# A two-layer network in one kernel: the layer's output kept in SBUF over the layer change, operand sums on one engine, an output projection begun earlier

## The chip, the cores and the metric

The kernel runs on one core of a Trainium2 chip. The metric is the device time of one execution in microseconds (us). Lower is better. Before the change it is 2079.74 us, the median of three runs (2078.81 to 2080.0).

## The reference, cut to what matters

One sequence of 1024 tokens with 1024 features goes through two layers in float32. The first (even) layer mixes by pooling, retention and attention to a memory of 256 tokens; the second (odd) by block-sparse attention with 12 heads ("NSA") and again by attention to the memory.

```python
def even_layer(h, mem_n, g, w_in, pool_w, pool_scale, w_mem_kv, w_out):
    u = rmsnorm(h, g)
    za, rq, rk, rv, xq, gate = split_cols(u @ w_in, EVEN_SPLITS)
    ...
    y = jnp.concatenate([a, r, m], axis=-1) * jax.nn.silu(gate)
    return h + y @ w_out

def odd_layer(h, mem_n, g, w_in, cmp_pe, cmp_w1, cmp_b1, cmp_w2, w_mem_kv, w_out, rel_bias):
    u = rmsnorm(h, g)
    q, kc, vc, ks, vs, kw, vw, gl, xq, gate = split_cols(u @ w_in, ODD_SPLITS)
    c = nsa_attention(q, kc, vc, ks, vs, kw, vw, gl, cmp_pe, cmp_w1, cmp_b1, cmp_w2, rel_bias)
    m = mem_attention(xq, mem_n, w_mem_kv)
    y = jnp.concatenate([c, m], axis=-1) * jax.nn.silu(gate)
    return h + y @ w_out
```

The change touches three places: the end of the first layer (`h + y @ w_out`), the start of the second (`rmsnorm`, and the operands of `u @ w_in`), and the start of the second layer's attention.

## The kernel before, in words

Activations are kept transposed, features on the 128 partitions and tokens along the free dimension, in two halves of 512 tokens (`hf` 0 and 1); a tensor of 1024 features is 8 tiles of 128x512 per half. PE (TensorE) does every product of a weight and an activation as three matmuls of 512 columns (L77 to L79), because each operand is split into a high part, which ACT casts (L70), and a low part, the difference, which DVE (VectorE) or POOL (GpSimd) computes (L71). A weight is loaded raw as `wr`, split into `wh` and `wl`, and then used.

The order in which each engine takes its instructions is not written out by hand: the program is traced in the order of the code, a scheduler reorders it with a model of times, and each engine then runs its own list strictly in order. DMAs are nearly all issued from SP's list, in order as well. Where an instruction waits, everything behind it on its engine waits too.

**The layer change.** `out_proj` (from L538, loop over `ct`, 8 output tiles) computes the first layer's output: 24 matmuls per tile into `ps_mm`, plus the residual `xr` (loaded from `hp`), stored to DRAM as `hd`; squares are summed into `hacc` for the norm. While the second half's `out_proj(1)` runs on PE, the first half is loaded from `hd`, scaled in place by its norm (L764), split into the operands B11 and B21, and stored again, scaled, to `xd` (L757 to L768).

The odd layer's projections multiply both halves of the tokens and both halves of the features by a scheme of the Strassen kind, with 7 products in place of 8 (`strassen`, L225). Its activation operands are B11, B21 (of the first half alone), B22 (of the second half alone) and T1 to T4 (sums and differences of both). `u_half` (L174) scales a half by its norm and makes the operands that need that half alone; `u_sums` (L181) makes T1 to T4. Six column groups (kc, vc, q0, q2, q4, q6) are begun with B11 and B21 alone (`early`, L203), 12 products of 12 matmuls each. Their order: the six `early` groups; then `mem_kv` (L295), the second layer's keys and values of the memory, which depends on nothing in the stream; then `u_half` of the second half and `u_sums`. The second half is loaded back from `hd`, the first from `xd`, 16 loads. `strassen` then goes through kc, vc, q and the rest, with weight sums `ws` on POOL (L231 to L234).

**The start of attention.** After the last projection, `kv_prep(0)` brings the keys and values, then `scores` of unit 0 (a head of a half) are computed, then for every unit `values` beside the next unit's `scores`. `od_out` (L831) is a generator of output products y·w (12 matmuls per step, 8 per half for this group), whose first group of four heads comes from the memory attention (`ymr` loaded from `ymd`). `proj_step` (L1262) takes one of its steps; it is called from the loop over units, so first beside unit 0's values.

## Time and profile before

| | |
|---|---|
| time, median of 3 runs | 2079.74 us (2078.81 to 2080.0) |
| the profiled execution's own time | 2074.93 us |
| its span in the trace | 2073.1 us |
| PE busy | 1945.5 us, 94% of the span |
| DVE, ACT, POOL busy | 1281.2, 943.2, 614.2 us (62%, 45%, 30%) |
| mean granted PE clock | 0.967 of full speed |
| DMA | 273.36 MB, 132 GB/s over the span |

The rows further down have, for an instruction, its start in us, its duration, engine, line, operation and tiles (output<-inputs), and in brackets how long the engine stood idle before it and what released it. A granted clock of 0.50 means that PE ran at 1.2 GHz in place of 2.4 GHz. Line numbers are those of the kernel before.

### The profile page before, as it was taken

The numbers are of one execution on the slowest core, as the hardware profiler recorded it, in microseconds if no ns is written. First come the engines' busy times: TensorE is split into PE (matmuls) and PEld (weight loads), VectorE is DVE, ScalarE is ACT, GpSimd is POOL, SyncE is SP. The second block draws the span as 40 slices with busy tenths as digits, with TensorE's granted clock in tenths as the row PEclk, the third lists the DMA queues.
The fourth block names the chain that finished last, engine by engine and source line by source line (L and its number), as shares of the span: only waits on it lengthen the run. The fifth ranks groups of instructions, "written<-read, shape, count | busy, mean of one in ns | idle before, by whom it ended". The sixth has DMA issues, their size and how long they took to land.

```text
span 2073.1 us, 28764 instructions
## 1 busy us (share of the span) xinstructions
PE 1945.5 (94%) x9814; PEld 1618.8 (78%) x9814; DVE 1281.2 (62%) x2729; ACT 943.2 (45%) x1867; POOL 614.2 (30%) x627
## 2 busy tenths in 40 slices
PE   5799999979999999849999999998999999999997
PEld 4688888858888877728878788886788888878885
DVE  4666465555655563484536965676575677767675
ACT  4444332334432243331123344545575677756664
POOL 0121110010311002174436643342344443333422
PEclk9899999989999999959999999999999999999998
DMA  6423234442232438517645443335536442152312
GB/s 202 155 81 102 82 110 134 160 138 92 84 104 82 157 130 279 191 47 219 211 129 164 157 136 129 129 120 182 190 120 203 161 132 62 34 166 62 108 41 91
DMA packets 131702, 273.36 MB, mean 132 GB/s; under 512 B 15927, under 2 KB 33091, under 8 KB 131523
## 3 DMA queue, kind: packets, MB, share of 16 engines
q1 hardware_dynamic: 131556, 271.53, 40.7%
q8 instruction: 77, 1.26, 0.3%
q14 instruction: 69, 0.57, 0.1%
HBM read 211.16 MB, written 62.66 MB: 132 GB/s over the span
## 4 chain that ended last, share of the span: by engine, by line
PE 48%; DVE 4%; POOL 2%; DMA 2%; issue 1%; ACT 1%; SPq 0%; DVEq 0%; POOLq 0%; ACTq 0%
PE ps_t L120 5%; PE ps_a L77 3%; PE ps_a L78 3%; PE ps_a L79 3%; PE ps_s L77 3%; PE ps_s L79 3%; PE ps_s L78 3%; PE ps_mm L79 3%; PE ps_mm L77 3%; PE ps_mm L78 3%; PE ps_o L84 2%; PE ps_o L82 2%; PE ps_o L83 2%; PE ps_b L77 2%; PE ps_b L79 2%; PE ps_b L78 2%
## 5 line engine op out<-in xcount | busy, mean ns | idle before, releaser
L70 ACT CAST wh<-wr 128x512 fp32r<-128x512 f32 (+1 forms) x395 | 242.2, 618 | 474.5 <-PE ps_mm L78 304.4
L71 DVE TENSOR_TENSOR wl<-wr,wh 128x512 fp32r<-128x512 f32 (+1 forms) x281 | 208.1, 745 | 175.9 <-ACT wh L70 168.9
L77 PE MATMUL ps_mm<-uh,wh 128*128 128x512 f32 x640 | 253.2, 398 | 2.7 <-ACT uh L70 2.7
L79 PE MATMUL ps_mm<-uh,wl 128*128 128x512 f32 x640 | 252.9, 395 | 0.0
L78 PE MATMUL ps_mm<-ul,wh 128*128 128x512 f32 x640 | 252.6, 395 | 0.0
L71 POOL TENSOR_TENSOR wl<-wr,wh 128x512 fp32r<-128x512 f32 x114 | 150.0, 1318 | 325.7 <-ACT wh L70 270.4
L79 PE MATMUL ps_mm<-yh,wl 128*128 128x512 f32 x512 | 205.4, 402 | 2.2 <-DVE wl L71 1.3
L77 PE MATMUL ps_mm<-yh,wh 128*128 128x512 f32 x512 | 203.2, 403 | 4.0 <-ACT wh L70 2.1
L78 PE MATMUL ps_mm<-yl,wh 128*128 128x512 f32 x512 | 204.4, 400 | 0.2 <-DVE yl L71 0.2
L71 DVE TENSOR_TENSOR apl<-ps_t,aph 128x512 fp32r<-128x512 f32 x204 | 135.9, 671 | 44.0 <-ACT aph L70 38.6
L70 ACT CAST aph<-ps_t 128x512 fp32r<-128x512 f32 x204 | 114.5, 567 | 86.7 <-PE ps_o L83 44.5
L77 PEld LDWEIGHTS ps_mm<-uh,wh 128*128 128x128 f32 x640 | 121.1, 190 | 28.3 <-ACT uh L70 4.4
L78 PEld LDWEIGHTS ps_mm<-ul,wh 128*128 128x128 f32 x640 | 121.1, 189 | 24.6 <-DVE ul L71 0.5
L79 PEld LDWEIGHTS ps_mm<-uh,wl 128*128 128x128 f32 x640 | 120.9, 189 | 24.6
L1201 POOL TENSOR_TENSOR Pw<-Pw,arc 128x640 f32<-128x640 f32 (+2 forms) x96 | 97.7, 1018 | 141.1 <-DVE arc L1197 65.4
L70 ACT CAST wh<-ws 128x512 fp32r<-128x512 f32 x88 | 54.2, 619 | 136.0 <-PE ps_a L78 63.0
L77 PEld LDWEIGHTS ps_mm<-yh,wh 128*128 128x128 f32 x512 | 95.7, 188 | 25.3 <-ACT wh L70 4.5
L79 PEld LDWEIGHTS ps_mm<-yh,wl 128*128 128x128 f32 x512 | 96.3, 188 | 24.0 <-POOL wl L71 2.6
L78 PEld LDWEIGHTS ps_mm<-yl,wh 128*128 128x128 f32 x512 | 96.3, 188 | 20.3 <-DVE yl L71 0.8
L71 DVE TENSOR_TENSOR wl<-ws,wh 128x512 fp32r<-128x512 f32 x88 | 71.2, 811 | 40.8 <-ACT wh L70 37.6
L1193 ACT ACTIVATE Ps<-Ps,anm 128x512 f32<-128x512 f32 (+3 forms) x96 | 74.6, 777 | 27.0 <-DVE anm L1190 26.7
L1203 ACT ACTIVATE Ps<-Ps,arc 128x512 f32<-128x512 f32 (+3 forms) x96 | 74.4, 777 | 21.6 <-DVE arc L1197 20.0
(891 smaller groups left out, 4863.6 us busy)
## 6 DMA issues: line engine op xcount, KB each, us to landing
wr<-in_ev_gate SPq DMA_DIRECT2D x32, 512.0 KB, 3.5
wr<-in_ev_out SPq DMA_DIRECT2D x32, 512.0 KB, 3.6
wr<-in_od_out SPq DMA_DIRECT2D x64, 256.0 KB, 3.2
oa<-oho SPq DMA_DIRECT2D x52, 256.0 KB, 2.5
oxr<-oa SPq DMA_DIRECT2D x52, 256.0 KB, 2.8
x<-in_xT SPq DMA_DIRECT2D x32, 256.0 KB, 3.7
wr<-in_od_q SPq DMA_DIRECT2D x16, 512.0 KB, 3.9
w<-in_cmp_w SPq DMA_DIRECT2D x16, 512.0 KB, 4.8
```

The lines of the kernel that those rows point to most:

```text
L70: act.copy(hi, src)
L71: (eng or dve).tensor_tensor(lo, src, hi.bitcast(F32), OP.subtract)
L77: pe.matmul(o, wh, xh, start=start, stop=False, skip_group_check=skip)
L78: pe.matmul(o, wh, xl, start=False, stop=False, skip_group_check=skip)
L79: pe.matmul(o, wl, xh, start=False, stop=stop, skip_group_check=skip)
L82: pe.matmul(o, wh, xh, start=start, stop=False)
L83: pe.matmul(o, wl, xh, start=False, stop=False)
L84: pe.matmul(o, wh, xl, start=False, stop=stop)
L120: pe.transpose(o, x, ident[:k, :k])
L1193: act.activation(pt, pt, AF.Exp, bias=nm[:, bi:bi + 1], accum_out=su[:, bi:bi + 1])
L1201: pool.tensor_tensor(pt, pt, rc[:, bi:bi + 1].to_broadcast(list(pt.shape)), OP.mult)
L1203: act.activation(pt, pt, AF.Copy, scale=rc[:, bi:bi + 1])
```

## The change: what it does

1. **The halves stay in SBUF.** A pool `xp` with 16 tiles X[f][k] is opened ahead of `out_proj(1)`. The first half's X[0] is loaded from `hd` and scaled in place by `u_half`; nothing is stored to `xd`. For the second half, `out_proj` loads the residual into X[1][ct] and adds the product in place, so that the half is in SBUF when the norm is known. 24 DMAs of 256 KB are gone: 8 stores to `xd`, 8 loads from it, 8 loads from `hd`. The squares get a tile of their own, `hsq`.
2. **Order and engines of the operands.** `u_half` of the second half and `u_sums` stand behind the first two `early` groups, ahead of the other four and of `mem_kv`. In `u_sums` every subtraction and every split's low half is on DVE (before, POOL had 8 subtractions and 4 of the splits' low halves, with T4's splits on DVE). T4's splits come after `mem_kv` (`u_last`).
3. **Start of attention.** One `proj_step` stands ahead of `kv_prep(0)`, and one in each step of unit 0's `scores`.
4. Pools are opened earlier or on the other side, and the tile `th` of a gate comes from another pool with two buffers.

```diff
@@ out_proj @@
-                    xr = ep.tile([128, HT], F32, name="xr", tag="xr", bufs=2)
+                    last = hf == 1 and not first
+                    xr = X[1][ct] if last else ep.tile([128, HT], F32, name="xr", tag="xr", bufs=2)
                     sp.dma_start(xr, a["xT"][ct][:, hf * HT:(hf + 1) * HT] if first else hp_[ct][hf])
-                    t = ep.tile([128, HT], F32, name="ho", tag="ho", bufs=2)
+                    t = xr if last else ep.tile([128, HT], F32, name="ho", tag="ho", bufs=2)
                     dve.tensor_tensor(t, o, xr, OP.add)
@@ u_sums @@
             dve.tensor_tensor(b11, b12, b11, OP.subtract)
-            pool.tensor_tensor(b12, b22, b12, OP.subtract)
+            dve.tensor_tensor(b12, b22, b12, OP.subtract)
             dve.tensor_tensor(b22, b22, b11, OP.subtract)
             split(*U["T2"][k], b22)
-        for k in range(4):
-            split(*U["T3"][k], x[1][k], eng=(dve, pool)[k % 2])
-        for k in range(4):
-            split(*U["T1"][k], x[0][k], eng=(dve, pool)[k % 2])
+            dve.tensor_tensor(x[0][k + 4], x[0][k + 4], b22, OP.subtract)
+        for nm, f in (("T3", 1), ("T1", 0)):
+            for k in range(4):
+                split(*U[nm][k], x[f][k])
+
+    def u_last(U, uo, x):
         U["T4"] = u_late(uo)
         for k in range(4):
-            pool.tensor_tensor(x[0][k + 4], x[0][k + 4], x[1][k + 4], OP.subtract)
             split(*U["T4"][k], x[0][k + 4])
@@ layer change @@
     for k in range(8):
-        x = ep.tile([128, HT], F32, name="x0", tag="pa", bufs=3)
-        sp.dma_start(x, hd[k][0])
-        dve.scalar_tensor_tensor(x, x, gains[:, 1, k:k + 1], rb, OP.mult, OP.mult)
-        split(*U[("B11", "B21")[k // 4]][k % 4], x)
-        sp.dma_start(xd[k], x)
+        sp.dma_start(X[0][k], hd[k][0])
+    u_half(U, X, 1, 0, rh[0], tm2.tile([128, HT], F32, name="rb", tag="rb"))
     out_proj(1, EV_ORDER[1], False)
...
-        ahead = [("kc", 0), ("vc", 0), ("q", 0), ("q", 2), ("q", 4), ("q", 6)]
...
-            if n == 0:
-                for k in range(8):
-                    sp.dma_start(X[1][k], hd[k][1])
-                    sp.dma_start(X[0][k], xd[k])
-        drain(mem_kv("od", None, u_late(uo), wtile("mrb")[:, :NMEM]))
-        u_half(U, X, 1, 1, rh[1], wtile("rb"))
-        u_sums(U, uo, X)
+    ahead(("kc", 0), ("vc", 0))
+    u_half(U, X, 1, 1, rh[1], wtile("rb"))
+    u_sums(U, X)
+    ahead(("q", 0), ("q", 2), ("q", 4), ("q", 6))
+    drain(mem_kv("od", None, u_late(uo), wtile("mrb")[:, :NMEM]))
+    u_last(U, uo, X)
@@ attention @@
+        proj_step()
         kv_prep(0)
         res = []
         for _ in scores(*units[0], res):
-            pass
+            proj_step()
         kv_prep(1)
```

The scheduler moves more than the code does. Three places, in the rows of the engines' lists, each with its tiles' numbers and what it waits for:

DVE at the start of `out_proj(1)`, where the low halves of the weights of output tile 0 are done (`wl_6626` before, `wl_6630` now). Before:

```order
L71 TENSOR_TENSOR wl_6622<-wr_6619,wh_6621 128x512 [waits DMAHW6_49,Activation_49]
L71 TENSOR_TENSOR wl_6626<-wr_6619,wh_6625 128x512 [waits Activation_49]
L71 TENSOR_TENSOR B110l_6547<-x0_6571,B110h_6546 128x512 [waits Activation_49]
L71 TENSOR_TENSOR B111l_6549<-x0_6577,B111h_6548 128x512 [waits Activation_49]
L71 TENSOR_TENSOR wl_6664<-wr_6661,wh_6663 128x512 [waits DMAHW7_49,Activation_49]
L71 TENSOR_TENSOR wl_6668<-wr_6661,wh_6667 128x512 [waits Activation_49]
```

Now:

```order
L178 SCALAR_TENSOR_TENSOR x05_6571<-x05_6571,c_gains_66,rb_6590 128x512 [waits DMAHW7_49]
L71 TENSOR_TENSOR B112l_6552<-x02_6568,B112h_6551 128x512 [waits Activation_49]
L178 SCALAR_TENSOR_TENSOR x06_6572<-x06_6572,c_gains_66,rb_6590 128x512 [waits DMAHW0_49]
L178 SCALAR_TENSOR_TENSOR x07_6573<-x07_6573,c_gains_66,rb_6590 128x512 [waits DMAHW1_49]
L71 TENSOR_TENSOR B113l_6554<-x03_6569,B113h_6553 128x512 [waits Activation_49]
L71 TENSOR_TENSOR B210l_6556<-x04_6570,B210h_6555 128x512 [waits Activation_49]
L566 TENSOR_TENSOR x10_6574<-ps_mm_6633,x10_6574 128x512 [waits DMAHW2_49,PE_49]
L71 TENSOR_TENSOR B211l_6558<-x05_6571,B211h_6557 128x512 [waits Activation_49]
L71 TENSOR_TENSOR wl_6667<-wr_6664,wh_6666 128x512 [waits DMAHW3_49,Activation_49]
L71 TENSOR_TENSOR wl_6671<-wr_6664,wh_6670 128x512 [waits Activation_49]
```

Between the low halves of tile 0 and those of tile 1 (`wl_6664` before, `wl_6667` now) stood two splits; now there stand 14 instructions: 7 scalings, 6 splits and the sum of tile 0, which needs its 24 matmuls done. The last ten of the 16 rows are shown.

DVE ahead of `mem_kv`, whose first weights' low half is `wl_7399` before and `wl_7424` now (T40h to T43l at L306 and L308 are the memory's operand there, in T4's tiles). Before:

```order
L306 SCALAR_TENSOR_TENSOR T42h_7365<-wr_7380,c_gains_66,T42h_7365 128x256 [waits DMAHW7_49,Activation_49]
L306 SCALAR_TENSOR_TENSOR T42l_7366<-wr_7380,c_gains_66,T42l_7366 128x256 [waits Activation_49]
L306 SCALAR_TENSOR_TENSOR T43h_7367<-wr_7380,c_gains_66,T43h_7367 128x256 [waits Activation_49]
L306 SCALAR_TENSOR_TENSOR T43l_7368<-wr_7380,c_gains_66,T43l_7368 128x256 [waits Activation_49]
L71 TENSOR_TENSOR wl_7399<-wr_7396,wh_7398 128x512 [waits DMAHW0_49,PE_49,Activation_49]
```

Now:

```order
L189 TENSOR_TENSOR x05_6571<-x05_6571,x15_6579 128x512 [waits DVE_49]
L308 SCALAR_TENSOR_TENSOR T42h_7390<-wr_7405,c_gains_66,T42h_7390 128x256 [waits DMAHW7_49,Activation_49]
L308 SCALAR_TENSOR_TENSOR T42l_7391<-wr_7405,c_gains_66,T42l_7391 128x256 [waits Activation_49]
L308 SCALAR_TENSOR_TENSOR T43h_7392<-wr_7405,c_gains_66,T43h_7392 128x256 [waits Activation_49]
L71 TENSOR_TENSOR T21l_6991<-x15_6579,T21h_6990 128x512 [waits Activation_49]
L71 TENSOR_TENSOR T22l_6993<-x16_6580,T22h_6992 128x512 [waits Activation_49]
L189 TENSOR_TENSOR x06_6572<-x06_6572,x16_6580 128x512
L308 SCALAR_TENSOR_TENSOR T43l_7393<-wr_7405,c_gains_66,T43l_7393 128x256
L189 TENSOR_TENSOR x07_6573<-x07_6573,x17_6581 128x512 [waits DVE_49]
L71 TENSOR_TENSOR T23l_6995<-x17_6581,T23h_6994 128x512 [waits Activation_49]
L71 TENSOR_TENSOR wl_7424<-wr_7421,wh_7423 128x512 [waits DMAHW2_49,Activation_49,Pool_49]
```

All of `u_half` and `u_sums` now stands ahead of `mem_kv`'s first weights on DVE: from the first scaling of the second half to `T23l` 50 instructions, 8 scalings, 16 subtractions, 16 splits, 8 of the memory's operand and 2 sums of `early` groups. The T1 to T4 products need nothing further from DVE but T4's splits.

PE at the start of attention, behind the last projection's transposes of values. Before:

```order
L120 MATMUL ps_t_12545<-c_ident_72,vraw_12543 128x128 x3
L77 MATMUL ps_s_12606<-ks0h_12511,aqh_12594 128x512 [waits Activation_49]
L78 MATMUL ps_s_12606<-ks0l_12512,aqh_12594 128x512 [waits DVE_49]
L79 MATMUL ps_s_12606<-ks0h_12511,aql_12595 128x512 [waits Pool_49]
L77 MATMUL ps_s_12612<-kw0h_12515,aqh_12594 128x512 [waits Activation_49]
```

Now:

```order
L120 MATMUL ps_t_12547<-c_ident_72,vraw_12545 128x128 x3
L77 MATMUL ps_mm_12523<-yh_12501,wh_12519 128x512 [waits Activation_49]
L77 MATMUL ps_mm_12634<-yh_12501,wh_12630 128x512 [waits DVE_49]
L78 MATMUL ps_mm_12523<-yl_12502,wh_12519 128x512 [waits DVE_49]
L79 MATMUL ps_mm_12523<-yh_12501,wl_12520 128x512 [waits Pool_49]
L77 MATMUL ps_mm_12523<-yh_12505,wh_12519 128x512 [waits Activation_49]
```

Two output products, 24 matmuls, now stand ahead of unit 0's first score on PE. The matmuls ahead of unit 0's values are as many as before.

## Rows read from the trace of the kernel before

**Rows 1.** The page: the span, and the busy time, share and instructions of each engine.

```profile
span 2073.1 us, 28764 instructions
PE 1945.5 (94%) x9814; PEld 1618.8 (78%) x9814; DVE 1281.2 (62%) x2729; ACT 943.2 (45%) x1867; POOL 614.2 (30%) x627
```

**Rows 2.** Busy time by stage: the stretch, its length, then busy us (and count) of PE, PEld, DVE, ACT and POOL, the granted PE clock, the DMA engines' busy share, GB/s. The first stretch is the start of `out_proj(1)`, then come the `early` groups, `mem_kv`, the operands of the second half, the first Strassen groups, and the start of attention in two parts.

```profile
760.00:812.00 52.00, 46.99 (x200) 36.67 (x198) 32.83 (x50) 23.11 (x40) 6.21 (x5) 1.00 0.73 244
812.00:846.00 34.00, 30.49 (x130) 24.85 (x130) 7.41 (x15) 10.79 (x22) 10.22 (x9) 0.95 0.77 273
846.00:875.00 29.00, 28.43 (x168) 25.01 (x168) 14.06 (x24) 10.07 (x18) 0.24 (x1) 1.00 0.70 218
875.00:929.00 54.00, 19.72 (x39) 10.29 (x39) 44.86 (x50) 17.83 (x31) 40.47 (x21) 0.61 0.16 53
929.00:974.00 45.00, 45.00 (x192) 36.01 (x193) 17.71 (x28) 8.18 (x14) 17.27 (x13) 0.90 0.73 219
1425.00:1436.00 11.00, 5.86 (x17) 3.85 (x16) 6.00 (x12) 4.11 (x7) 2.55 (x2) 0.69 0.96 311
1436.00:1476.00 40.00, 34.07 (x165) 26.31 (x165) 25.04 (x66) 25.07 (x58) 21.56 (x24) 0.97 0.89 307
```

**Rows 3.** What PE waited for from 760 to 975 us: PE's tile and line, who released it, total us, times, the longest.

```profile
PE ps_b L77 <- ACT T10h L70: 8.4, 1, 8.4
PE ps_b L78 <- POOL T11l L71: 6.3, 1, 6.3
PE ps_b L78 <- DVE T10l L71: 5.2, 1, 5.2
PE ps_t L154 <- DVE dg L149: 4.4, 1, 4.4
PE ps_a L77 <- DVE u L242: 4.1, 1, 4.1
PE ps_a L78 <- DVE T20l L71: 2.9, 1, 2.9
PE ps_t L134 <- DVE hacc L128: 2.7, 1, 2.7
PE ps_s L77 <- ACT wh L70: 2.6, 1, 2.6
...
PE ps_a L79 <- DVE wl L71: 2.0, 1, 2.0
```

**Rows 4.** Short stretches, columns as in rows 2: one behind the wait at 813 us, one behind the wait at 846 us, three of the operands' stage.

```profile
816.00:818.00 2.00, 2.00 (x6) 1.51 (x6) 0.00 (x0) 0.00 (x0) 0.00 (x0) 0.50 1.00 368
844.00:848.00 4.00, 1.51 (x10) 1.30 (x11) 3.43 (x7) 2.73 (x6) 0.00 (x0) 1.00 0.41 110
880.00:900.00 20.00, 3.53 (x6) 1.13 (x4) 16.31 (x23) 8.69 (x15) 13.47 (x5) 0.50 0.16 53
900.00:920.00 20.00, 11.37 (x22) 5.90 (x22) 20.00 (x13) 6.51 (x11) 20.00 (x12) 0.59 0.00 0
920.00:940.00 20.00, 15.13 (x50) 11.14 (x51) 8.88 (x16) 2.94 (x5) 4.76 (x4) 0.67 0.36 113
```

**Rows 5.** DVE, in order of time: a step of the memory's operand, then scalings of the second half, subtractions, and a split of T2.

```profile
836.26 0.48 DVE L306 SCALAR_TENSOR_TENSOR T40h<-wr,c_gains,T40h 128x256 fp32r<-128x256 f32 x1 [6.13 <-ACT T40h L305]
...
881.74 6.39 DVE L177 SCALAR_TENSOR_TENSOR x<-x,c_gains,rb 128x512 f32<-128x512 f32 x8 [2.48 <-ACT rb L157]
888.05 1.88 DVE L184 TENSOR_TENSOR x<-x,x 128x512 f32<-128x512 f32 x3
...
908.85 1.75 DVE L71 TENSOR_TENSOR T20l<-x,T20h 128x512 fp32r<-128x512 f32 x1
```

**Rows 6.** POOL, in order of time: the first weight sum behind `mem_kv`, a weight's split, a weight sum, and a split of T3.

```profile
874.76 1.26 POOL L231 TENSOR_TENSOR ws<-wr 128x512 f32<-128x512 f32 x1 [35.46 <-DMA wr<-in_od_kc]
...
883.85 1.74 POOL L71 TENSOR_TENSOR wl<-wr,wh 128x512 fp32r<-128x512 f32 x1 [5.27 <-ACT wh L70]
888.27 8.81 POOL L234 TENSOR_TENSOR ws<-wr,ws 128x512 f32<-128x512 f32 x1 [2.68 <-DVE x L177]
...
908.34 1.71 POOL L71 TENSOR_TENSOR T31l<-x,T31h 128x512 fp32r<-128x512 f32 x1
```

**Rows 7.** The start of `out_proj(1)`: PE's first matmul with a low weight, DVE's low halves for tile 1, and DVE's sum of tile 0.

```profile
765.80 0.50 PE L79 MATMUL ps_mm<-yh,wl 128*128 128x512 f32 x1 [1.28 <-DVE wl L71]
...
767.48 1.29 DVE L71 TENSOR_TENSOR wl<-wr,wh 128x512 fp32r<-128x512 f32 x2
...
774.51 0.68 DVE L563 TENSOR_TENSOR ho<-ps_mm,xr 128x512 f32<-128x512 f32 x1
```

**Rows 8.** PE: the first and the last of the 12 matmuls of one `early` product, and the end of the first Strassen groups, where the compressed keys begin.

```profile
826.44 0.39 PE L77 MATMUL ps_c<-B210h,wh 128*128 128x512 f32 x1
...
828.93 0.39 PE L79 MATMUL ps_c<-B213h,wl 128*128 128x512 f32 x1
...
973.59 1.50 PE L934 MATMUL ps_s<-kp,w 128*128 128x126 f32 x12
```

**Rows 9.** The start of attention: PE's first score, SP's issue of two of the four loads of the memory attention's output, and the transposes of values that waited last.

```profile
1430.38 0.80 PE L77 MATMUL ps_s<-ks0h,aqh 128*128 128x512 f32 x1 [4.56 <-ACT ks0h L70]
...
1474.55 1.08 PE L120 MATMUL ps_t<-c_ident,vraw 128*128 128x128 f32 x4 [3.14 <-DMA vraw<-ovw]
...
1430.43 0.90 SPq L837 DMA_DIRECT2D ymr<-ymd  x2
```

More of the change, by code (lines that the diff above doesn't have):

```diff
@@ L120, in transpose, with add_square @@
         pe.transpose(o, x, ident[:k, :k])
-    def add_square(acc, x, n, first, eng=None):
+    def add_square(acc, x, n, first, eng=None, sq=None):
         if first:
@@ L125, in add_square @@
         else:
-            sq = tmp.tile([128, n], F32, name="sq", tag="uf", bufs=2)
+            if sq is None:
+                sq = tmp.tile([128, n], F32, name="sq", tag="uf", bufs=2)
             act.activation(sq, x, AF.Square)
@@ L179, in u_half, with u_sums @@
                 split(*U[("B11", "B21", "", "B22")[2 * f + k // 4]][k % 4], x[f][k])
-    def u_sums(U, uo, x):
+    def u_sums(U, x):
         for k in range(4):
@@ L413, in sink @@
             z = c if o is None else o
-            th = p_.tile([128, HT], F32, name="th", tag="th", bufs=cur["th"])
+            th = tmp.tile([128, HT], F32, name="th", tag="uf", bufs=2)
             act.activation(th, z, AF.Tanh, scale=0.5)
@@ L567, in out_proj @@
                             acc = ep.tile([128, HT], F32, name="hacc", tag="hacc")
-                        add_square(acc, t, HT, ct == 0)
+                        add_square(acc, t, HT, ct == 0, sq=ep.tile([128, HT], F32, name="hsq", tag="hsq"))
                 if not first:
@@ L759, in net @@
     U = u_pool(uo, ("B11", "B21"))
-    rb = spread(rh[0], HT, r=tm2.tile([128, HT], F32, name="rb", tag="rb"))
+    xpx = ExitStack()
+    xp = xpx.enter_context(tc.tile_pool(name="xp", bufs=1, side="right", reuse_waits="tile"))
+    X = [[xp.tile([128, HT], F32, name=f"x{f}{k}") for k in range(8)] for f in range(2)]
     for k in range(8):
-        x = ep.tile([128, HT], F32, name="x0", tag="pa", bufs=3)
-        sp.dma_start(x, hd[k][0])
-        dve.scalar_tensor_tensor(x, x, gains[:, 1, k:k + 1], rb, OP.mult, OP.mult)
-        split(*U[("B11", "B21")[k // 4]][k % 4], x)
-        sp.dma_start(xd[k], x)
+        sp.dma_start(X[0][k], hd[k][0])
+    u_half(U, X, 1, 0, rh[0], tm2.tile([128, HT], F32, name="rb", tag="rb"))
     out_proj(1, EV_ORDER[1], False)
@@ L770, in net @@
     psum("ps0", a=2, b=1, c=1, s=2, t=2)
-    uo = uox.enter_context(tc.tile_pool(name="uo1", bufs=1, side="right", reuse_waits="tile"))
+    kvs = ctx.enter_context(tc.tile_pool(name="kvs", bufs=1, reuse_waits="tile"))
+    ulx = ExitStack()
+    uo = ulx.enter_context(tc.tile_pool(name="uo1", bufs=1, reuse_waits="tile"))
     U.update(u_pool(uo, ("T3", "T1", "T2", "B22")))
@@ L785, in net, with ahead @@
     kd = {}
-    with tc.tile_pool(name="xp", bufs=1, reuse_waits="tile") as xp:
-        X = [[xp.tile([128, HT], F32, name=f"x{f}{k}") for k in range(8)] for f in range(2)]
-        ahead = [("kc", 0), ("vc", 0), ("q", 0), ("q", 2), ("q", 4), ("q", 6)]
-        for n, (nm, i) in enumerate(ahead):
+    st = ulx.enter_context(tc.tile_pool(name="st1", bufs=1, reuse_waits="tile"))
+    def ahead(*names):
+        for nm, i in names:
             sink, sc_ = od_dst(nm, i)
             kd[nm, i] = early(U, a["od_" + nm][i], sink,
-                              lambda: xp.tile([128, HT], F32, name="p1", tag="p1", bufs=2),
-                              lambda: xp.tile([128, HT], F32, name="sc", tag="sc", bufs=2), sc_)
-            if n == 0:
-                for k in range(8):
-                    sp.dma_start(X[1][k], hd[k][1])
-                    sp.dma_start(X[0][k], xd[k])
-        drain(mem_kv("od", None, u_late(uo), wtile("mrb")[:, :NMEM]))
-        u_half(U, X, 1, 1, rh[1], wtile("rb"))
-        u_sums(U, uo, X)
+                              lambda: st.tile([128, HT], F32, name="p1", tag="hs", bufs=cur["hs"]),
+                              lambda: st.tile([128, HT], F32, name="sc", tag="sc", bufs=cur["sc"]), sc_)
+    ahead(("kc", 0), ("vc", 0))
[4 more added lines that the diff above has]
+    u_last(U, uo, X)
+    xpx.close()
     def mem_heads(p_, pre, xq, gate, dst, bufs=1, pbufs=1):
@@ L813, in mem_heads @@
                 yield
-    kvs = ctx.enter_context(tc.tile_pool(name="kvs", bufs=1, reuse_waits="tile"))
     gts = kvs.tile([128, 8, 36], F32, name="gts")
@@ new lines, in net, with proj_pair, gate_pair @@
+    p_ = st
+    def proj_pair(nm, i):
+        sink, sc_ = od_dst(nm, i)
+        strassen(U, a["od_" + nm][i], a["od_" + nm][i + 1], sink, p_, sc_, kd.get((nm, i)))
+    def gate_pair(i):
+        strassen(U, a["od_gate"][i], a["od_gate"][i + 1], gate_sink(p_, sgd[i], sgd[i + 1]), p_)
+    proj_pair("kc", 0)
+    proj_pair("vc", 0)
+    proj_pair("q", 0)
+    rel_tables()
+    proj_pair("q", 2)
+    compress()
+    proj_pair("q", 4)
+    gates_in(p_)
+    for i in (6, 8, 10):
+        proj_pair("q", i)
+        rel_rows(i // 2 - 3)
@@ new lines, in net @@
+    proj_pair("xq", 0)
+    rel_rows(3)
+    select()
+    proj_pair("xq", 2)
+    rel_rows(4)
+    for i in (12, 14):
+        gate_pair(i)
+    rel_rows(5)
+    proj_pair("ks", 0)
+    with tc.tile_pool(name="mx1", bufs=1, reuse_waits="tile") as mp_:
+        g = mem_heads(mp_, "od", zo["xq"], sgd, ymd)
+        for nm in ("kw", "vs", "vw", 0, 2, 4, 6, 8, 10):
+            next(g, None)
+            if isinstance(nm, str):
+                proj_pair(nm, 0)
+            else:
+                gate_pair(nm)
+        flush()
+        drain(g)
@@ L1084, in net @@
+    ulx.close()
     uox.close()
```

37 lines of the change are left out of this document (removed).

## The prediction, made before the changed kernel ran

> **What bounds the kernel now.** I read the page first: PE is busy 94% of a span of 2073.1 us [rows 1]. So over most of the span only less PE work helps, and this change takes none away. What it can win is time in which PE stands or runs at half clock. Next I read the busy times by stage [rows 2]. Of the stages that the change touches one stands out: from 875 to 929 us PE is busy 19.72 of 54 us, at a granted clock of 0.61, while DVE is busy 44.86 and POOL 40.47. PE waits there for the operands of the second half. Ahead of it, in `mem_kv`, PE is busy 28.43 of 29 us and DVE only 14.06; from 812 to 846 DVE is busy 7.41 of 34. The work that PE waits for could have been done there.
>
> The waits say for what [rows 3]. T10h, T11l, T10l, the norm's `dg`, `u`, T20l and one `wl` follow on `mem_kv` one upon another: 8.4 + 6.3 + 5.2 + 4.4 + 4.1 + 2.9 + 2.0 = 33.3 us. What PE did between them ran slowly: 3.53 us busy at 0.50, 11.37 at 0.59, 15.13 at 0.67 [rows 4], so 3.53 x 0.50 + 11.37 x 0.41 + 15.13 x 0.33 = 11.4 us were lost to the clock. Both together, 44.7 us, are the most that an earlier second half can give.
>
> **The change, part by part.**
>
> *The loads and stores that go* (24 of 256 KB). Their stage has the DMA engines at 0.77 and PE at 30.49 of 34 us [rows 2]; the waits there are for the norm's sum and a cast [rows 3]. I price them at nothing by themselves; what they give is that the second half needs no landing before it is scaled. The cover is PE's `early` products, and its loss would cost the 2.6 us that PE now waits for the cast at 846.
>
> *The operands, earlier.* The norm's sum is ready at about 814. In the new list the norm's broadcast stands on PE behind three `early` products of 2.88 us each (826.44 to 828.93 + 0.39 [rows 8]), with 1 to 2 us for the clock, which is at 0.50 behind the wait at 813 [rows 4]. With ACT's copy, DVE can scale from about 826. Its 50 instructions cost, undisturbed: 8 scalings and 2 sums at 6.39 / 8 = 0.80, 32 subtractions and splits at 1.88 / 3 = 0.63, 8 memory steps at a bit under 0.48 [rows 5], so 8.0 + 20.2 + 3.6 = 31.8 us, until about 858. The first low weights of `mem_kv` stand behind them on DVE, and PE behind these. PE has 12 `early` products, 34.6 us, of which two come within `mem_kv`; it reaches `mem_kv` at about 814 + 10 x 2.88 + 1.5 = 844 to 848 and waits there for **some 10 us**, where it waits 2.6 now [rows 3]: a cost of 7.4. Ends: 0, if the list leaves room for PE's work, and 14.
>
> *Behind `mem_kv`* all of T1 to T3 and B22 are ready, so the 33.3 us go, but for one thing that is late next: the weights of kc. POOL's first weight sum starts at 874.76, as `mem_kv` ends, released by its load [rows 6]; three sums of 1.26 and a cast and a split of some 0.6 each come to 5 us. The loads may come earlier now, as SP's list is shorter. I take 3; ends 0 and 5.
>
> *The clock.* A wait may cost the clock for a while: 0.50 behind the 2.7 us at 813, 1.00 behind the 2.6 us at 846 [rows 4]. For three new waits (here, at the kc weights, and in the next part) I take 4 us in all, between 0 and the 11.4 lost now.
>
> *`out_proj(1)`'s start.* Between the low weights of tile 0 and of tile 1 DVE now has 14 instructions where it had two: 7 x 0.80 + 7 x 0.63 = 10.0 us. It goes on from 766.4, when the split that released PE at 765.80 and the next one are done [rows 7], to about 776.4, and one split more brings 777. PE has 24 matmuls for tile 0, 5.8 us, so it is out of work at about 771. In the kernel before, those splits ended at 768.8 [rows 7]. That would be a stall of 6 us; but DVE has two scalings fewer ahead of tile 0, 1.6 us, and the first matmuls of tile 1 need only high weights. I take **3.5**; ends 0 and 6. Later tiles have slack: DVE is busy 32.83 of 52 us there [rows 2].
>
> *POOL beside DVE.* Seven low halves of weights for q0 to q6 are on POOL while DVE has its run of 50. Each row alone shows one price. From 900 to 920 DVE and POOL are both busy without a break [rows 4], a T2 split of DVE takes 1.75 and a POOL split 1.71 [rows 5, 6], where 0.63 and 1.26 are their times otherwise: one POOL instruction costs DVE about 1.1 us. Seven make **7.5**, which lengthen DVE's run and with it PE's wait. But at 888.27 a POOL sum takes 8.81 us [rows 6], while DVE subtracts at its full pace of 0.63 [rows 5]: POOL gets nothing until DVE pauses. Then PE's products wait for POOL, and DVE, at its second `early` sum, for PE; this pause lets POOL in. By that the price is 13 (rival 2). The low end is 0. I take 7.5, since most of DVE's instructions here wait for a cast of ACT's, as those at 908 do, and not those at 888.
>
> The Trainium skill, "SBUF — State Buffer", section "Who interferes with whom", says that a DVE instruction with two SBUF inputs contends with a GpSimd one that reads SBUF, and that whoever issues first holds the shared pair "for the whole instruction", the other blocking fully. A lock of one instruction would give the alternation of 900 to 920 and a price of 7.5; the 8.81 us at 888.27 are longer than any one DVE instruction there, and no rule of that section gives them.
>
> *DVE for POOL in `u_sums`*: 8 subtractions and 4 splits more on DVE, in the 31.8 above; what POOL is spared lay beside it.
>
> *Start of attention.* PE now takes 24 matmuls of y·w, 5.8 us, ahead of the first score (1430.38 [rows 9]); their input was issued at 1430.43 [rows 9], so the score may be as much as 11 us later. The matmuls up to unit 0's values are as many as before, PE is busy 34.07 of the last 40 us, the DMA engines 0.96 and 0.89 [rows 2], and the last wait is for values still to be loaded, 3.14 us at 1474.55 [rows 9]. Loads bound this stretch either way. I take a loss of **1.5**; ends a gain of 4.6 (the first wait filled [rows 9]) and a loss of 11.
>
> *Pools, `th`, `hsq`* change buffers that no wait in rows 3 is for: nothing; their cover is the slack of DVE and ACT.
>
> **Sum.** 44.7 - 7.4 - 3 - 4 - 3.5 - 7.5 - 1.5 = 17.8, so about 18 us gained. The profiled execution took 2074.93 us, 1.8 more than its span; it would take 2057. The median of the runs, 2079.74, is 4.8 above it, so the forecast is 2079.74 - 18 = **2062 us**. A measurement of this kernel can tell about 0.2%, 4.2 us, from no change.
>
> **The rivals.**
>
> 1. *Full cover.* PE reaches `mem_kv` as its weights come, POOL costs nothing, the clock holds: 44.7 - 3 - 3.5 = 38 us, **2042**. For it: the scheduler's list interleaves the memory's operand with the sums. Against it: the 50 instructions are a chain through DVE of 31.8 us, and the products beside it are 28.8.
> 2. *POOL starved.* 13 in place of 7.5, and 6 for the late `out_proj`: 18 - 5.5 - 2.5 = 10, **2070**. For it the 8.81 us; against it the 900 to 920 stretch.
> 3. *Scores late.* The 11 us at the start of attention come through in full: 18 - 9.5 = 8, **2071**. For it: the scores' softmax follows on them. Against it: the last wait is a load's.
> 4. *Slower: PE cut off behind POOL.* The second low half of q0 and those of q2 get through on POOL only when DVE's run ends, at about 858. PE is out of products at about 831 and stands for 27 us where I have 10 and POOL's 7.5: about 10 more. It then runs the seven products left, 20.2 us, at half clock as it did from 880 to 900 [rows 4], another 20 less the 4 in the sum. 18 - 10 - 16 = -8, **2088**. It decides at 834: if POOL has q2's first low half by then, it is not this. For it the 8.81 us; against it DVE's own wait for an `early` sum, which gives POOL room.
> 5. *Nothing moves:* the operands are bound by ACT's casts or by the norm, and PE waits as long elsewhere: within 4 us of 2080. DVE, not ACT, is the busy one from 875 to 929 (44.86 against 17.83 [rows 2]).
>
> **How the numbers follow.** The forecast (2049 to 2067, the sum's own terms varied) 0.49; rival 1 0.17; rival 2 0.13; rival 3 0.07; rival 4 0.09; rival 5 0.05. The first four cases are faster by over 4.2 us: 0.86; rival 5 is the same: 0.05; rival 4 is slower: 0.09. The range is 2040 to 2075: it takes in rivals 1 to 3 and leaves out rivals 4 and 5, 0.14, and the tail of rival 1 below its 2042.
>
> **What would show it.** Right: the waits for T10h, T11l, T10l and T20l are gone, PE is busy over 45 of the 54 us behind `mem_kv` at a clock over 0.85, and `mem_kv`'s first matmul waits 5 to 15 us for `wl` on DVE or its cast; the compressed keys (973.59 [rows 8]) begin at 950 to 960. Also a wait of 2 to 6 us at `out_proj(1)`'s second tile, and unit 0's values as far from the last projection as now, within 4 us. POOL's splits in DVE's run of 1.7 us speak for the forecast, of 5 or more for rivals 2 or 4. Wrong: a sum of PE's waits from 760 to 960 that is no smaller than the 38.6 of rows 3, or half clock throughout `mem_kv`.

## The result, and the profile after

The changed kernel takes 2048.81 us, the median of four runs (2047.62 to 2052.55), beside 2079.87 us for the kernel before (2078.81 to 2081.12): a ratio of 0.9854, with a 95% interval from 0.9836 to 0.9871. That is 31 us less, where 18 were forecast; it lies inside the range. The profiled execution took 2047.62 us, 27.3 less than the profiled one of before.

The page, first line and busy times, against [rows 1]: PE does the same work (1944.2 for 1945.5 us) in a shorter span.

```profile
span 2045.8 us, 28686 instructions
PE 1944.2 (95%) x9814; PEld 1618.4 (79%) x9814; DVE 1276.0 (62%) x2741; ACT 943.0 (46%) x1867; POOL 598.7 (29%) x615
```

Stages of the kernel after, columns as in [rows 2]: start of `out_proj(1)`; norm and the first `early` groups; the rest of DVE's run, where PE waits; `mem_kv`; the first product of the Strassen groups; the groups behind it; the start of attention.

```profile
745.00:801.00 56.00, 52.41 (x211) 40.66 (x210) 33.49 (x56) 23.10 (x39) 4.00 (x4) 0.94 0.60 211
801.00:835.00 34.00, 29.50 (x130) 23.21 (x128) 22.22 (x36) 15.16 (x30) 16.56 (x10) 1.00 0.36 116
835.00:846.00 11.00, 5.49 (x12) 3.80 (x12) 11.00 (x20) 5.75 (x13) 2.18 (x1) 0.69 0.55 192
846.00:881.00 35.00, 31.21 (x168) 27.20 (x168) 19.10 (x33) 12.37 (x22) 0.78 (x1) 0.90 0.55 173
881.00:890.00 9.00, 6.14 (x14) 4.32 (x14) 6.41 (x8) 3.36 (x6) 6.61 (x5) 0.62 0.52 160
890.00:924.00 34.00, 33.64 (x157) 26.22 (x156) 14.10 (x22) 6.79 (x12) 15.93 (x12) 1.00 0.85 247
1406.00:1451.00 45.00, 36.76 (x174) 30.24 (x173) 25.00 (x70) 26.22 (x58) 21.17 (x24) 0.88 0.89 296
```

The stage that was slowest before (19.72 of 54 us busy at 0.61 [rows 2]) has no counterpart: behind `mem_kv` PE waits for under 4 us in all (3.2 and, at 920, 0.4). What PE waited for from 760 to 960 us, as [rows 3]:

```profile
PE ps_c L77 <- DVE sc L220: 6.0, 1, 6.0
PE ps_a L77 <- ACT wh L70: 3.2, 1, 3.2
PE ps_s L79 <- DVE wl L71: 2.9, 1, 2.9
PE ps_t L135 <- DVE hacc L129: 2.4, 1, 2.4
PE ps_s L77 <- ACT wh L70: 1.5, 1, 1.5
PE ps_mm L79 <- DVE wl L71: 0.9, 1, 0.9
PE ps_a L79 <- POOL wl L71: 0.7, 1, 0.7
```

Five of [rows 3] are gone altogether (T10h, T11l, T10l, T20l, `u`); the norm's `dg` is made while PE has products to do. In their place stand 6.0 us for the sum of an `early` group, which frees the bank that the next such product writes, and 1.5 and 2.9 us for `mem_kv`'s first weights.

**Where the time came from.** The two traces can be laid side by side at matmuls that both have. The 2000th matmul starts at 479.66 us before and 468.98 after: 10.7 us were won in the *first* layer, in a place of which the prediction did not speak. The wait is PE's longest in the first 750 us but for the start; of before and of after:

```profile
PE ps_t L134 <- DVE acc L128: 24.8, 2, 14.6
```

```profile
PE ps_t L135 <- DVE acc L129: 15.7, 1, 15.7
```

Two times before, once after. The wait that went, in the trace of before, with ACT's squares ahead of it:

```profile
427.80 0.63 ACT L127 ACTIVATE sq<-ho 128x512 f32<-128x512 f32 x1 [0.34 <-DVE ho L563]
428.33 0.61 ACT L127 ACTIVATE sq<-x 128x512 f32<-128x512 f32 x1
...
437.14 1.84 PE L134 MATMUL ps_t<-ones,acc 128*128 128x1 f32 x8 [10.16 <-DVE acc L128]
```

The squares of the second half's input (`sq<-x`) start half a microsecond after the last square of the first half's output (`sq<-ho`). After, `sq<-x` runs 263 us earlier:

```profile
164.87 1.14 ACT L128 ACTIVATE sq<-x 128x512 f32<-128x512 f32 x2
```

From the first low-weight matmul of `out_proj(1)` (765.80 [rows 7], 754.59 after) the lead is 11.2 us; at the norm's sum (about 813 and 805.53) 7.6; at the end of the last projection (1425.38 and 1394.51) 30.9; at the transposes for unit 0's values (1475.42 and 1450.19) 25.2; at the end of the span 27.3. So: first layer +10.7, `out_proj(1)` about -3, from the norm's sum to the end of the projections +23.3, the start of attention -5.6, the rest +2. The +23.3 are themselves a gain of some 26 at the operands and a loss of 2.8 further on, where the same matmuls take longer (last section).

### The profile page after: what moved, and what is told of

Same layout as the page of the kernel before. It is cut to its first block, busy times and chain, and to the rows that moved or that the text cites. A ratio compares the mean times of both kernels' runs of the same rounds, so it can differ in the third digit from the quotient of the medians.

```text
span 2045.8 us, 28686 instructions
## 1 busy us (share of the span) xinstructions
PE 1944.2 (95%) x9814; PEld 1618.4 (79%) x9814; DVE 1276.0 (62%) x2741; ACT 943.0 (46%) x1867; POOL 598.7 (29%) x615
## 3 DMA queue, kind: packets, MB, share of 16 engines
q8 instruction: 77, 1.26, 0.3%
## 4 chain that ended last, share of the span: by engine, by line
PE 48%; DVE 3%; DMA 2%; issue 1%; ACT 1%; POOL 0%; SPq 0%; DVEq 0%; POOLq 0%; ACTq 0%
PE ps_t L120 5%; PE ps_a L77 3%; PE ps_a L78 3%; PE ps_a L79 3%; PE ps_s L77 3%; PE ps_mm L77 3%; PE ps_mm L79 3%; PE ps_s L78 3%; PE ps_s L79 3%; PE ps_mm L78 3%; PE ps_o L84 2%; PE ps_o L83 2%; PE ps_o L82 2%; PE ps_b L77 2%; PE ps_b L78 2%; PE ps_b L79 2%
## 5 line engine op out<-in xcount | busy, mean ns | idle before, releaser
L71 DVE TENSOR_TENSOR wl<-wr,wh 128x512 fp32r<-128x512 f32 (+1 forms) x281 | 213.8, 766 | 173.6 <-ACT wh L70 167.7
L71 POOL TENSOR_TENSOR wl<-wr,wh 128x512 fp32r<-128x512 f32 x114 | 158.6, 1393 | 325.4 <-ACT wh L70 292.2
L79 PEld LDWEIGHTS ps_mm<-yh,wl 128*128 128x128 f32 x512 | 97.5, 191 | 23.3 <-DVE wl L71 2.6
L71 DVE TENSOR_TENSOR wl<-ws,wh 128x512 fp32r<-128x512 f32 x88 | 68.2, 776 | 59.1 <-ACT wh L70 55.7
```

The lines of the kernel that those rows point to most:

```text
L71: (eng or dve).tensor_tensor(lo, src, hi.bitcast(F32), OP.subtract)
L79: pe.matmul(o, wl, xh, start=False, stop=stop, skip_group_check=skip)
```

## The experiments

All ratios are to the kernel before, run on the same chip as the variant. The last row of the table is the fastest version of all.

| variant | us | ratio | 95% interval |
|---|---|---|---|
| the change | 2048.81 | 0.9854 | 0.9836 to 0.9871 |
| the change, beside the `th` variants | 2047.29 | 0.9869 | 0.9848 to 0.9889 |
| before, with `hsq` | 2063.2 | 0.9945 | 0.9929 to 0.9961 |
| change without `hsq` | 2060.11 | 0.9925 | 0.9905 to 0.9945 |
| operands late again | 2070.17 | 0.9966 | 0.9952 to 0.998 |
| second half reloaded | 2050.33 | 0.9867 | 0.985 to 0.9883 |
| most of POOL's share of the sums back | 2055.22 | 0.989 | 0.9875 to 0.9906 |
| `mem_kv`'s key weights on POOL | 2053.67 | 0.9895 | 0.9874 to 0.9917 |
| change without the `proj_step` calls | 2047.26 | 0.9863 | 0.9843 to 0.9883 |
| before, with the `proj_step` calls | 2080.64 | 1.0019 | 1.0005 to 1.0032 |
| `th` apart | 2044.79 | 0.9853 | 0.9831 to 0.9876 |
| `th` apart, no `proj_step` calls | 2043.76 | 0.9852 | 0.9829 to 0.9874 |
| `th` apart, calls in the scores alone | 2038.63 | 0.9814 | 0.9798 to 0.9831 |

### The gain in the first layer: two tiles shared by two stages

In the kernel before, a square goes into a tile `sq` of the pool `tmp` under the tag `uf`, which has two buffers; every other user of that tag takes its turn on them in the order of the program. The first half's `out_proj` stands ahead of the second half's input norm in the program, so the norm's squares cannot take a buffer until the output's squares have had theirs. One edit to the kernel before:

```diff
-                        add_square(acc, t, HT, ct == 0)
+                        add_square(acc, t, HT, ct == 0, sq=ep.tile([128, HT], F32, name="hsq", tag="hsq"))
```

> The kernel before, with one edit: the squares of the output projection get a tile of their own (hsq) in place of one of the two shared tiles. Theory A: the squares of the second half's input norm stood behind the output projection's squares only because both take the same two tiles in turn; with a tile of their own the wait of 10.2 us for acc at 437 us goes and the time falls by 9 to 11 us, to about 2069.5. Theory B: that wait went because of the other edits (pools, kept halves): within 2 us of 2079.9.

Measured 2063.2 us, 0.55% or 11.4 us less by the ratio, a little more than theory A said; PE's waits from 380 to 500 us no longer hold one for `acc`; the longest is:

```profile
PE ps_t L155 <- DVE dg L150: 2.8, 1, 2.8
```

The opposite edit takes `hsq` out of the changed kernel.

> The changed kernel without hsq: the squares take the shared tiles again. Theory A: the 10.2 us wait for acc comes back and the time rises by 9 to 11 us, to about 2059. Theory B: the time stays within 2 us of 2048.8.

Measured 2060.11 us, and the wait is back (from 380 to 500 us):

```profile
PE ps_t L135 <- DVE acc L129: 9.9, 1, 9.9
```

Both ways theory A holds: the tile is worth some 11 us by itself (10.7 in the traces, 11.4 by the first ratio, 11.3 by the medians of the change with and without it), and nothing else of the change is needed for it.

### The gain at the layer change: place or residence?

The operands go back behind all `early` groups and `mem_kv`; halves in SBUF and sums on DVE stay:

```diff
-    ahead(("kc", 0), ("vc", 0))
-    u_half(U, X, 1, 1, rh[1], wtile("rb"))
-    u_sums(U, X)
-    ahead(("q", 0), ("q", 2), ("q", 4), ("q", 6))
+    ahead(("kc", 0), ("vc", 0), ("q", 0), ("q", 2), ("q", 4), ("q", 6))
     drain(mem_kv("od", None, u_late(uo), wtile("mrb")[:, :NMEM]))
+    u_half(U, X, 1, 1, rh[1], wtile("rb"))
+    u_sums(U, X)
     u_last(U, uo, X)
```

> The changed kernel with the operands of the second half put back behind the six early groups and the memory's keys and values; the halves stay in SBUF and all sums stay on DVE. Theory A: the place of the operands is the gain at the layer change; PE waits again for over 20 us behind mem_kv, part of it at half clock, and the time rises by 15 to 25 us, to 2064 to 2074. Theory B: that the halves are in SBUF is the gain; the time rises by under 6 us, to 2049 to 2055.

Measured 2070.17 us: 21 us more than the change (23 by the ratios), inside theory A's span. Waits of [rows 3] are back; the two largest now:

```profile
PE ps_b L77 <- ACT T10h L70: 8.4, 1, 8.4
PE ps_b L78 <- DVE T10l L71: 7.0, 1, 7.0
```

Then the other part alone: the order of the change, but the second half is summed into `ho` and loaded back in 8 loads.

```diff
-                    last = hf == 1 and not first
+                    last = False
...
     out_proj(1, EV_ORDER[1], False)
+    for k in range(8):
+        sp.dma_start(X[1][k], hd[k][1])
```

> The changed kernel, but the output projection of the second half adds into a tile of its own, and the half is loaded back from memory in 8 loads behind it; the first half is kept, and the order of the operands is as in the changed kernel. Theory A: the loads land by about 822 us, some 6 us behind the point at which DVE now begins to scale (816.4), DVE's run ends that much later, and PE's wait ahead of mem_kv grows: the time rises by 3 to 7 us, to 2052 to 2056. Theory B: the norm's way to DVE hides the loads, and the time stays within 2 us of 2048.8.

Measured 2050.33 us, within 2 us of the change (theory B). DVE starts to scale at 817.56 where it did at 816.42, and for the same reason, ACT's copy of the norm:

```profile
817.56 2.86 DVE L178 SCALAR_TENSOR_TENSOR x<-x,c_gains,rb 128x512 f32<-128x512 f32 x4 [3.44 <-ACT rb L158]
```

My 6 us for the landing were wrong, because the output projection stores and reloads each tile as it goes: the last reload is issued at 806, as the norm is being summed. So the place of the operands is the gain, and holding the second half in SBUF adds nothing that these runs can tell. What was not tried is the early place with the first half reloaded too. The run with the late place bounds it: by the ratio that kernel is 7 us faster than the one before, while the tile `hsq` alone is worth 11, so that both halves in SBUF, with the sums on DVE, can be worth there no more than what the rest of the change costs.

### DVE alone, or DVE with POOL

POOL gets most of its old share of `u_sums` back: four of its eight subtractions, and every second low half of T3 and T1, 8 instructions.

```diff
-            dve.tensor_tensor(b12, b22, b12, OP.subtract)
+            pool.tensor_tensor(b12, b22, b12, OP.subtract)
...
-                split(*U[nm][k], x[f][k])
+                split(*U[nm][k], x[f][k], eng=(dve, pool)[k % 2])
```

> The changed kernel with POOL's old share of the operand sums: four subtractions and every second low half of T3 and T1 on POOL again. Theory A: POOL and DVE hinder each other, so the work given back to POOL does not shorten DVE's run of 32.8 us; the early groups' splits on POOL wait behind it, PE waits longer ahead of mem_kv, and the time rises by 2 to 8 us (2051 to 2057). Theory B: DVE's run is shortened by the 8 instructions, some 4 to 5 us, and the time falls to 2044 to 2047.

Measured 2055.22 us: 4 to 8 us more than the change's two results, as theory A has it. DVE and POOL in the middle of the run:

```profile
832.37 1.75 DVE L71 TENSOR_TENSOR T10l<-x,T10h 128x512 fp32r<-128x512 f32 x1
834.04 3.44 DVE L187 TENSOR_TENSOR x<-x,x 128x512 f32<-128x512 f32 x2
...
828.45 6.79 POOL L186 TENSOR_TENSOR x<-x,x 128x512 f32<-128x512 f32 x4
```

Every instruction of these rows takes 1.7 us. From the first scaling to T23l DVE needs 35.1 us for 38 instructions (8 are on POOL, and 4 of the memory's operand now stand behind T23l), where the change needs 32.8 for 50; and PE waits 6.1 us for one `early` weight on POOL:

```profile
PE ps_a L79 <- POOL wl L71: 6.7, 2, 6.1
```

DVE and POOL in the changed kernel:

```profile
816.42 4.18 DVE L178 SCALAR_TENSOR_TENSOR x<-x,c_gains,rb 128x512 f32<-128x512 f32 x6 [3.44 <-ACT rb L158]
...
821.85 2.48 DVE L185 TENSOR_TENSOR x<-x,x 128x512 f32<-128x512 f32 x4
...
825.94 1.79 DVE L71 TENSOR_TENSOR B221l<-x,B221h 128x512 fp32r<-128x512 f32 x1
...
848.58 0.68 DVE L71 TENSOR_TENSOR T23l<-x,T23h 128x512 fp32r<-128x512 f32 x1
...
821.19 7.68 POOL L71 TENSOR_TENSOR wl<-wr,wh 128x512 fp32r<-128x512 f32 x3 [4.45 <-ACT wh L70]
833.41 3.77 POOL L71 TENSOR_TENSOR wl<-wr,wh 128x512 fp32r<-128x512 f32 x1 [4.54 <-ACT wh L70]
```

Most of DVE's run is at 0.60 to 0.62 us an instruction, with four POOL splits in it. The rows of [rows 5, 6] are both seen again: at 821.85 DVE keeps its pace (four in 2.48 us) while the first of POOL's three splits stands for 4.28 us; at 825.94 both take turns. The rule of the Trainium skill that was weighed, in "SBUF — State Buffer", section "Who interferes with whom", agrees with the turns (1.7 us each) and says nothing of why POOL is kept out over several instructions. (What the prediction quotes from the Trainium skill of a whole instruction stands there for DVE's two-port modes; for two SBUF inputs the section says that the engines contend, under one exclusive lock.)

The other way round, `mem_kv`'s first eight low halves on POOL:

```diff
-            w = wload(a[pre + "_mk"][h])
+            w = wload(a[pre + "_mk"][h], eng=None if first else pool)
```

> The changed kernel with the low halves of mem_kv's eight key weights on POOL in place of DVE. Theory A: PE's waits of 1.47 and 2.94 us at the start of mem_kv, and part of the 5.98 us for the early group's sum, come from DVE's run of 50 instructions; with the weights on POOL mem_kv starts up to 4 us earlier, and the time falls by 2 to 5 us (2044 to 2047). Theory B: POOL does not get its turn beside DVE's run (one split took 3.77 us at 833), so the wait only changes its name: within 2 us of 2048.8, or slower.

Measured 2053.67 us, 6 us more than the change on the same chip: theory B. In part the waits change their name and stay:

```profile
PE ps_c L77 <- DVE sc L220: 6.0, 1, 6.0
...
PE ps_s L77 <- ACT wh L70: 3.1, 2, 1.7
PE ps_s L79 <- POOL wl L71: 2.7, 1, 2.7
```

The wait for `wh` could not move: in the changed kernel the first of these weights is loaded only at 839.90, when DVE's run has read the raw tile of the memory's operand for the last time (T41l, until 839.85), and it lands at 845.77; with the splits on POOL it is 840.23 and 845.27.

### The loss at the start of attention

The first suspect is the change's third part. The edit takes both calls out of the changed kernel:

```diff
-        proj_step()
         kv_prep(0)
         res = []
         for _ in scores(*units[0], res):
-            proj_step()
+            pass
```

> The changed kernel without the two proj_step calls at the start of attention. Theory A: the output products ahead of the first scores and their loads ahead of the keys and values cost 3 to 5 us net, so about 2044.5, with the first score at most 6 us behind the last projection and unit 0's values 50 us behind it. Theory B: the work done earlier is missing later, and the time stays within 2 us of 2048.8. Theory C: the calls pay, and the time rises to over 2051.

Measured 2047.26 us, a ratio of 0.9863: theory B. The calls together neither cost nor give what can be told, and without them unit 0's values still begin 54.2 us behind the last projection (55.7 with them, 50.0 before). So most of the 5.6 us lost were not theirs. The first keys and values were loaded early in the trace before, the first two rows here, and late in the trace after, the others:

```profile
1213.96 0.32 SPq L401 DMA_DIRECT2D kraw<-oks  x1
1252.05 0.32 SPq L401 DMA_DIRECT2D vraw<-ovs  x1
...
1394.96 0.38 SPq L403 DMA_DIRECT2D kraw<-oks  x1
1397.13 0.38 SPq L403 DMA_DIRECT2D vraw<-ovs  x1
...
1395.33 0.63 ACT L417 ACTIVATE th<-sc 128x512 f32<-128x512 f32 x1 [2.66 <-DVE sc L254]
...
1400.78 1.12 PE L120 MATMUL ps_t<-c_ident,vraw 128*128 128x128 f32 x4 [6.27 <-DMA vraw<-ovs]
```

After, the first keys and values are loaded only as the last gates' tanh (`th`) is done, and PE stands 6.27 us for them. `kraw` and `vraw` are tiles of the tag `uf` too; and the change has put `th` there (its part 4). It is the first layer's mechanism the other way round. `th` goes into two buffers of its own, in the space that X leaves:

```diff
-            th = tmp.tile([128, HT], F32, name="th", tag="uf", bufs=2)
+            th = cur["thp"].tile([128, HT], F32, name="th", tag="th", bufs=2)
...
     xpx.close()
+    cur["thp"] = uox.enter_context(tc.tile_pool(name="thp", bufs=1, side="right", reuse_waits="tile"))
```

> The changed kernel with the gates' tile th in a pool of its own (two buffers, in the space that the kept halves leave), in place of the two shared tiles. Theory A: at the start of attention the first keys and values (kraw, vraw) come from the two tiles that th now turns over, so their loads wait for the last gate; with th apart they are loaded ahead again, PE's wait of 6.27 us for vraw goes, and the time falls by 3 to 6 us against the changed kernel (2043 to 2046). Theory B: the loads are bound by the DMA engines and the output products ahead of the scores; the wait only moves, and the time stays within 2 us of 2048.8.

The loads move 218 and 179 us ahead, and unit 0's values begin at 1442.95, 7.2 us earlier than in the profile of the change and 49.5 us behind the last projection, as in the kernel before (50.0):

```profile
1177.23 0.32 SPq L403 DMA_DIRECT2D kraw<-oks  x1
1218.58 0.32 SPq L403 DMA_DIRECT2D vraw<-ovs  x1
...
1399.37 0.87 PE L120 MATMUL ps_t<-c_ident,vraw 128*128 128x128 f32 x3 [5.50 <-DMA vraw<-ovw]
1405.21 1.22 PE L77 MATMUL ps_mm<-yh,wh 128*128 128x512 f32 x2 [4.76 <-ACT yh L70]
...
1442.95 1.06 PE L120 MATMUL ps_t<-c_ident,pcf 128*64 128x128 f32 x4
```

The time is 2044.79 us. The changed kernel ran beside it:

> The changed kernel itself, for comparison on the same chip: a ratio to the kernel before of 0.984 to 0.987.

It took 2047.29 us. The medians are 2.5 us apart and the intervals overlap, so the mechanism is shown by the loads, and its size, some 6 us at this place, by the trace alone. Theory A has the loads right and most of the time; but as theory B says, a wait is left: PE's first one is now for the second values, which are still issued at the end. Then the same without the two calls, and without the first of them:

```diff
-        proj_step()
         kv_prep(0)
```

> As the run before it, and the two proj_step calls at the start of attention are left out. Theory A (th blocks the loads, the calls cost up to 2 us): 2041 to 2045. Theory B (the calls pay once the keys come early): above the run before it by 2 us or more.

> The changed kernel with th in a pool of its own and without the proj_step ahead of the keys, but with the one in each step of unit 0's scores. Theory A: the leading products only fill PE's wait for the second values, so the time is within 2 us of the kernel with both calls (ratio 0.983 to 0.987 to the kernel before). Theory B: without them the scores begin some 5 us earlier and the time falls by 2 to 4 us more.

Without calls 2043.76 us, no different: theory A. With the calls in the scores alone 2038.63 us, a ratio of 0.9814, and the fastest version. That is the direction of theory B and more than its 2 to 4 us by the medians (6), but it ran on another chip than the kernel with both calls, and the two intervals just meet at 0.983. The first score begins 6.6 us earlier than with both calls (1406.20 for 1412.85), because it does not stand behind 24 matmuls that wait for `ymr`; the span of the profile is 2.1 us shorter. Unit 0's values begin 2.9 us earlier, in part because ten matmuls fewer stand ahead of them:

```profile
1440.08 0.60 PE L120 MATMUL ps_t<-c_ident,pcf 128*64 128x128 f32 x4
```

Last, the two calls put into the kernel before, with nothing else of the change:

> The kernel before with the two proj_step calls at the start of attention and nothing else of the change. Theory A: where the first keys and values are loaded early, the calls are worth nothing either way: within 3 us of the kernel before, unit 0's values within 3 us of their time there. Theory B: the output products ahead of the scores cost what the changed kernel lost at this place, 4 to 6 us.

Measured 2080.64 us, 0.19% more (interval 0.05 to 0.32%): between the theories. From the last projection to unit 0's values it takes 51.9 us in place of 50.0, and its first wait is for the weights of the products that now stand first:

```profile
1437.02 0.79 PE L77 MATMUL ps_mm<-yh,wh 128*128 128x512 f32 x1 [7.85 <-ACT wh L70]
...
1480.62 1.06 PE L120 MATMUL ps_t<-c_ident,pcf 128*64 128x128 f32 x4
```

So by the traces the leading `proj_step` costs some 2 us. That the calls in the scores pay rests on the run with them alone beside the one without any (2043.76), again on two chips.

## Why the prediction was right, and where it was wrong

**The main mechanism was right.** 33.3 us of waits and 11.4 of half clock behind `mem_kv` went, for the operands' earlier place, and the run with the late place shows that this is the cause. Of the signs named, PE is busy 50.78 of the 54 us behind `mem_kv` (881 to 935) at 0.94, where over 45 at over 0.85 was asked, and its waits from 760 to 960 sum to 18 us for 38.6. Other signs did not come: unit 0's values stand 5.6 us further from the last projection, not within 4, and the compressed keys begin at 923.46 and not at 950 to 960, since they now stand one column group earlier in PE's list, a move that the prediction did not see. Term by term:

- *The wait ahead of `mem_kv`, some 10 us*: 5.98 + 1.47 + 2.94 = 10.4 us, but with POOL's share in it, which the prediction adds as 7.5 more: 17.5 for the same wait, 7 too much. The larger part stands a little earlier than I put it, at an `early` product that waits for a bank, since the sum that frees it is in DVE's run as well.
- *The kc weights, 3 us*: 3.24.
- *POOL beside DVE, 7.5 us*: too much. DVE's run took 32.8 us from 816.42 to T23l; at the pace of its undisturbed rows here (0.66 a scaling, 0.60 a subtraction or split, 0.40 a memory step) it is 29.0, so POOL cost about 3.8. Only four of its splits fell into the run: eight of the twelve for the `early` groups were done by 816.74, as DVE began. And the 0.80 us a scaling of the prediction was no undisturbed pace: of the 6.39 us for eight in [rows 5], one took 1.75 beside POOL's split of [rows 6] at 883.85, and the others follow each other at 0.66.
- *The clock, 4 us*: too little. In the three stages of PE's new waits the granted clock was 0.69, 0.90 and 0.62 (835 to 890 us, above), which costs 5.49 x 0.31 + 31.21 x 0.10 + 6.14 x 0.38 = 7.2, so 3.2 more.
- *`out_proj(1)`, 3.5 us*: the size agrees with the 3 us lost between the two profiles, and the reason does not. PE's stall at tile 1 is 0.95 us, since DVE started earlier and its scalings ran at 0.67. The rest is clock, as the last section shows, and the unchanged code has it in other runs too.
- *The removed loads, nothing*: so it was for the second half's.

With the measured terms the operands give 44.7 - (10.4 - 2.6) - 3.2 - 7.2 = 26.5 us, where the sum had 44.7 - 7.4 - 3 - 4 - 7.5 = 22.8. Behind them 2.8 us are lost in the projections, for which the sum has no term. So it is luck that the stretch from `out_proj(1)` to the end of the projections agrees, 19.3 in the sum and 23.3 - 3 = 20 in the profiles.

**The step that failed** is the one that read "Pools, `th`, `hsq` change buffers that no wait in rows 3 is for: nothing". Rows 3 went from 760 to 975 us; the edit to `add_square` works wherever `out_proj` is used, in the first half too, and there it took away a wait of 10.16 us. And `th`, for which the same sentence said nothing, kept the first keys and values from being loaded ahead. I priced edits by the waits near them, in place of asking for each tag who else takes its buffers, in the whole program. The forecast of 18 us lacks the first (some 11 us) and has nothing for the second; its 1.5 at the start of attention stood for other work. The change without `hsq` took 2060.11 us, 2 from the forecast of 2062, but by errors that cancel. That the measured time lies 13 us below the forecast is, for some 11 of them, this tile's gain, which no term of the prediction names: luck, in a range that was wide.

*Start of attention, -1.5*: measured -5.6, for another reason than the one given. The products ahead of the first score cost about 2 us (the traces of the run with them in the scores alone, and of the one in the kernel before); what was lost beside that was the early load, and with `th` apart the place costs nothing against before.

**The rivals.** Full cover (1) did not come: PE waits 10 us ahead of `mem_kv`, although the time came near it through the first layer. POOL starved (2, 4): a POOL split took up to 4.28 us beside DVE, yet PE never stood for one longer than 0.65 us; q2's half was ready, which is where I had put the point of decision. Rival 3's 11 us: 5.6.

**The two baselines.** The profiled execution of before is 4.9 us below the median of its runs, that of after 1.2 below. So the medians are 31 us apart and the profiles 27; some 2 us of that difference is the clock at `out_proj(1)`. Of the fourteen profiles only that of before held it at full speed there: from the first low weight to the norm's sum it took 47.3 us, and in two of its variants 49.3 and 49.8.

## What to carry to other kernels

A tag with few buffers that several stages share is an order of work: each user waits for the user ahead of it in the program, however far apart the engines are. When an edit moves one tile in or out of such a tag, list every other user of it, in the whole program, and look for those whose work could run earlier; here one 256 KB tile was worth some 11 us, and another cost 6 us at its place in the trace, 2.5 by the medians. And move operands into the stretch where their engine idles before thinking about which loads to save: place gave 21 us, the second half's residence nothing that can be told.
